# Moving 22 operand tiles of an encoder layer to staggered places in SBUF

## The chip, the cores and the metric

The kernel runs on one core of a Trainium2 chip. The metric is device time in microseconds (us) for one call; lower is better. Times of 1 ns to 1 us are given in ns.

## What is computed

One layer of a bidirectional encoder on a sequence of 256 rows of width 2048: a gated feed-forward block (FFN 1), a mixer (eight heads of attention beside a convolution, joined by one output projection), and a second feed-forward block (FFN 2). All is in float32, and nearly all the arithmetic is in large matrix products against weights that are read once:

```
h = modulate(rms_norm(x, ffn1_pre_g), sh1, sc1)
x = x + 0.5 * g1 * rms_norm(silu(h @ w_gate) * (h @ w_up) @ w_down, ffn1_post_g)
h = modulate(rms_norm(x, mix_pre_g), sh2, sc2);  proj = h @ w_in
merged = concatenate([rms_norm(attention(q, k, v)), rms_norm(conv(u))]) @ w_out
x = x + g2 * rms_norm(merged, mix_post_g)
(the second feed-forward block as the first, with sh3, sc3, g3)
```

`w_gate` and `w_up` are 2048x5632, `w_down` is 5632x2048, `w_in` 2048x5120, `w_out` 2048x2048. The nine modulation vectors come from a vector-matrix product with `w_ada`, 2048x18432.

## The kernel before, in words

**Products.** A float32 operand is split into a high and a low part, both in the type float32r, and a product is made of three: high by high, high by low, low by high. The activations stand still in TensorE's array (the stationary operand, 128x128), the weights stream past (the moving operand, 128x512). In `Group.products`, for each of the 128-deep slices k and each half t of the 256 rows, three matmuls follow each other:

```
L312  matmul(o, xh, h)     stationary: high part of the activations
L313  matmul(o, xh, l)     the same stationary operand, loaded once more
L314  matmul(o, xl, h)     stationary: low part of the activations
```

I call these three a triple. Each matmul has a weight load of its own ahead of it (PEld in the profile). A chunk of weights is two slices; `wchunk` brings it in by DMA (tile `raw`), ScalarE rounds it to `hi` (L286), and VectorE subtracts for `lo` (L287).

**Where the stationary operands lie.** The high and low parts live in tiles of 128 partitions by 4 KB, made by `slot` from the pool `work`, one place per tag: `hh0` to `hh3` and `hl0` to `hl3` hold the normalized activations (`h1`, `h2`, `h3` in tile names), four slices each; `ah0` to `ah5` and `al0` to `al5` hold the hidden activations of the feed-forward blocks (`a_0h`, `a_1l` and so on); `fs0` to `fs3` hold sums and outputs, and in the mixer the first attention parts. A slice and half start at a multiple of 512 bytes inside a tile. The tags are also reused for float32 sums, attention tiles and the convolution. The tags `ah5` and `al5` alone are larger (`SLOT` words, 4576 bytes), for the padded convolution input.

The places in the built program, as bytes in a partition modulo 256, are these. All moving operands (`hi`, `lo`) start at byte 64.

```
tag              before   after          tag          before   after
hh0 hh1 hh2 hh3    0      0 64 128 192   hl0 to hl3     0      32 96 160 224
ah0 ah1 ah2 ah3    0      0 64 128 192   al0 to al3     0      32 96 160 224
ah4                0      128            al4            0      160
ah5                0      192            al5          224      160
fs0 fs2            0      0 64           fs1 fs3        0      32 96
```

So before, the tile `al5` is the only stationary operand of a triple that is not at byte 0. It holds the low part of the last hidden block of each round of the feed-forward blocks, and stands in 128 of the 2560 triples: at the end of each pass of the down projection (line L314 with `pd_t`), in runs of eight triples.

**Order.** One engine's instructions run in the order in which the Python code issues them; the tile framework adds the waits. While products run, background lanes (`tick`) put in the modulation sums for a later block on VectorE (L190), and their transposes on TensorE.

Of the kernel before, what the change touches and what calls it, by code (L numbers as in the profile page):

```python
# [16 lines left out]
P = 128  # L17
D = 2048
S = 256
# [32 lines left out]
RAW = 7  # L52
HILO = 4
SLOT = 4 * (S + 2 * PAD)

STAGES1 = ((0, 4), (4, 8), (8, 12), (12, 16))
STAGES2 = ((0, 4), (4, 10), (10, 16))
# [3 lines left out]
def encoder_layer(ctx, tc, a, consts, out):  # L61
# [5 lines left out]
    work = ctx.enter_context(tc.tile_pool(name="work", bufs=1))  # L67
# [164 lines left out]
    def gate_tile(gc, i):  # L232

        G = [slot(f"a{p}4", [P, NT, BLK], f"G{i}{p}") for p in "hl"]
        for n in range(0, D, BLK):
            ps = tr_ps(f"psg{i}_{n}")
            for j in range(BLK // P):
                g = gc[:, n // P + j:n // P + j + 1]
                nc.tensor.matmul(ps[:, j * P:(j + 1) * P], g.to_broadcast([P, P]), ident,
                                 start=True, stop=True)  # L240
            nc.scalar.copy(G[n // MW][:, n % MW // BLK, :], ps)
        return G


    def slot(tag, shape, name, dt=F32):

        n = int(np.prod(shape[1:]))
        t = work.tile([P, SLOT if tag in ("ah5", "al5") else 4 * S], dt, tag=tag, name=name)[:, :n]
        if len(shape) == 3:
            t = t.rearrange("p (a b) -> p a b", b=shape[2])  # L250
        elif len(shape) == 4:
            t = t.rearrange("p (a b c) -> p a b c", b=shape[2], c=shape[3])
        return t

    class Parts:
# [8 lines left out]
        def put(self, n, hi, lo):  # L264
            for parts, tag, p in ((self.hi, hi, "h"), (self.lo, lo, "l")):
                parts.extend([None] * (n + 1 - len(parts)))
                parts[n] = slot(tag, [P, 4, S], f"{self.base}{p}{n}", F32R)
# [121 lines left out]
    def f_tiles(i, tags=("fs0", "fs1", "fs2", "fs3")):  # L389
        return [slot(tag, [P, NT, BLK], f"f{i}_{db}") for db, tag in enumerate(tags)]  # L390
# [557 lines left out]
```

## Time and profile before

| | before |
|---|---|
| median of three runs | 1969.43 us (1967.24 to 1972.84) |
| the profiled execution | 1970.16 us |
| its span, first to last instruction | 1968.4 us |
| TensorE busy with matmuls | 1881.0 us, 96% |
| VectorE busy | 1474.6 us, 75% |
| ScalarE busy | 932.5 us, 47% |

The profile is of one execution. Recorded matmuls overlap, since the end of one is modelled; how fast products follow each other is read from the distance between their starts, which I call the pitch. PE is TensorE, DVE VectorE, ACT ScalarE, POOL GpSimd, SP the engine that issues most transfers.

### The profile page before, as it was taken

What the parts mean: (1) busy time and instruction counts of PE and PEld (TensorE: products, weight loads), DVE (VectorE), ACT (ScalarE), POOL (GpSimd) and SP (SyncE); (2) the same over time, 40 slices, a digit from 0 to 9 for tenths busy, and PEclk for the clock granted to TensorE, in tenths of its full rate; (3) what the DMA queues carried; (4) which work ended last, traced back from release to release, by engine and by line L of the source; (5) the groups of instructions that cost most, each with busy time, mean ns of one, the idle gap of its engine ahead of it and who ended that gap; (6) DMA issues with size and microseconds to landing.
All of it is one profiled execution on the core that took longest, in us unless ns stands there. A gap on an engine that the chain in (4) does not pass through costs nothing.

```text
span 1968.4 us, 23857 instructions
## 1 busy us (share of the span) xinstructions
PE 1881.0 (96%) x8451; PEld 1534.9 (78%) x8451; DVE 1474.6 (75%) x1824; ACT 932.5 (47%) x1437; POOL 64.1 (3%) x90
## 2 busy tenths in 40 slices
PE   2999999999999999899999997999999999999997
PEld 1888887888888878688887786888888777888886
DVE  6799999777787766689997768999885455444455
ACT  3554454444444444644455656635444433444442
POOL 2000000000000000000100000000000000000000
PEclk9999999999999999899999998999999999999999
DMA  9989988999999887356655667998777666656552
GB/s 335 324 298 310 332 273 275 352 328 325 322 319 332 303 273 260 115 183 185 180 163 194 207 201 244 341 333 299 238 232 234 217 228 226 201 186 189 175 190 99
DMA packets 249431, 493.12 MB, mean 251 GB/s; under 512 B 17065, under 2 KB 42433, under 8 KB 249312
## 3 DMA queue, kind: packets, MB, share of 16 engines
q1 hardware_dynamic: 247888, 491.38, 74.8%
q8 instruction: 66, 1.08, 0.2%
q14 instruction: 53, 0.43, 0.1%
q0 software_dynamic: 1248, 0.15, 0.1%
q10 hardware_dynamic: 176, 0.07, 0.0%
HBM read 489.44 MB, written 2.10 MB: 250 GB/s over the span
## 4 chain that ended last, share of the span: by engine, by line
PE 79%; DMA 10%; DVE 6%; issue 2%; ACT 2%; POOL 0%; SPq 0%; DVEq 0%; POOLq 0%; ACTq 0%
DMA ada<-in_w_ada 8%; PE pg_t L312 8%; PE pg_t L313 8%; PE pg_t L314 8%; PE pu_t L314 7%; PE pu_t L312 7%; PE pu_t L313 7%; PE pd_t L313 6%; PE pd_t L314 6%; PE pd_t L312 6%; PE pc_t L312 2%; PE pc_t L314 2%; PE pc_t L313 2%; DVE acc L190 2%; DVE lo_d L287 2%
## 5 line engine op out<-in xcount | busy, mean ns | idle before, releaser
L190 DVE SCALAR_TENSOR_TENSOR acc<-ada,cact,acc 128x512 f32<-128x512 f32 (+2 forms) x448 | 393.4, 899 | 145.9 <-DMA ada<-in_w_ada 136.0
L286 ACT CAST hi_d<-raw_d 128x1024 fp32r<-128x1024 f32 x176 | 184.8, 1051 | 268.8 <-PE pd_t L314 220.4
L286 ACT CAST hi_g<-raw_g 128x1024 fp32r<-128x1024 f32 x176 | 185.0, 1052 | 232.3 <-PE pg_t L314 129.6
L287 DVE TENSOR_TENSOR lo_d<-raw_d,hi_d 128x1024 fp32r<-128x1024 f32 x176 | 212.4, 1223 | 107.0 <-ACT hi_d L286 106.6
L286 ACT CAST hi_u<-raw_u 128x1024 fp32r<-128x1024 f32 x176 | 184.5, 1052 | 216.0 <-PE pu_t L314 100.7
L287 DVE TENSOR_TENSOR lo_u<-raw_u,hi_u 128x1024 fp32r<-128x1024 f32 x176 | 213.3, 1222 | 84.0 <-ACT hi_u L286 83.5
L287 DVE TENSOR_TENSOR lo_g<-raw_g,hi_g 128x1024 fp32r<-128x1024 f32 x176 | 213.7, 1222 | 73.2 <-ACT hi_g L286 73.1
L313 PE MATMUL pd_t<-lo_d,a_0h 128*128 128x512 f32 x384 | 151.3, 394 | 7.2 <-DVE lo_d L287 7.2
L314 PE MATMUL pd_t<-hi_d,a_0l 128*128 128x512 f32 x384 | 151.2, 394 | 0.0
L312 PE MATMUL pd_t<-hi_d,a_0h 128*128 128x512 f32 x384 | 150.3, 393 | 0.0
L312 PE MATMUL pg_t<-hi_g,h3h 128*128 128x512 f32 x352 | 140.0, 398 | 2.0 <-ACT h3h L353 2.0
L313 PE MATMUL pg_t<-lo_g,h3h 128*128 128x512 f32 x352 | 138.5, 393 | 1.4 <-DVE lo_g L287 1.4
L312 PE MATMUL pg_t<-hi_g,h1h 128*128 128x512 f32 x352 | 139.2, 396 | 0.0
L312 PE MATMUL pu_t<-hi_u,h3h 128*128 128x512 f32 x352 | 138.8, 395 | 0.0
L312 PE MATMUL pu_t<-hi_u,h1h 128*128 128x512 f32 x352 | 138.8, 395 | 0.0
L313 PE MATMUL pu_t<-lo_u,h3h 128*128 128x512 f32 x352 | 138.0, 392 | 0.8 <-DVE lo_u L287 0.8
L314 PE MATMUL pg_t<-hi_g,h3l 128*128 128x512 f32 x352 | 138.7, 394 | 0.0
L313 PE MATMUL pg_t<-lo_g,h1h 128*128 128x512 f32 x352 | 138.4, 393 | 0.0
L314 PE MATMUL pg_t<-hi_g,h1l 128*128 128x512 f32 x352 | 138.3, 393 | 0.0
L314 PE MATMUL pu_t<-hi_u,h3l 128*128 128x512 f32 x352 | 138.3, 393 | 0.0
L314 PE MATMUL pu_t<-hi_u,h1l 128*128 128x512 f32 x352 | 138.2, 393 | 0.0
L313 PE MATMUL pu_t<-lo_u,h1h 128*128 128x512 f32 x352 | 137.9, 392 | 0.1
(257 smaller groups left out, 3601.8 us busy)
## 6 DMA issues: line engine op xcount, KB each, us to landing
ada<-in_w_ada SPq DMA_DIRECT2D x288, 512.0 KB, 5.5
raw_g<-in_ffn_w_gate SPq DMA_DIRECT2D x176, 512.0 KB, 5.0
raw_u<-in_ffn_w_up SPq DMA_DIRECT2D x176, 512.0 KB, 4.9
raw_d<-in_ffn_w_down SPq DMA_DIRECT2D x176, 512.0 KB, 5.4
raw_c<-in_w_in SPq DMA_DIRECT2D x64, 256.0 KB, 3.0
raw_q<-in_w_in SPq DMA_DIRECT2D x16, 512.0 KB, 3.8
raw_k<-in_w_in SPq DMA_DIRECT2D x16, 512.0 KB, 3.6
raw_v<-in_w_in SPq DMA_DIRECT2D x16, 512.0 KB, 3.6
```

Of the source, the lines that this page charges most:

```text
L190: nc.vector.scalar_tensor_tensor(acc, w[:, j, :], cact[:, j0 + j:j0 + j + 1], acc, op0=ALU.mult, op1=ALU.add)
L286: nc.scalar.copy(h, r)
L287: nc.vector.tensor_tensor(l, r, f32(h), op=ALU.subtract)
L312: nc.tensor.matmul(o, xh, h, start=self.first and k == 0, stop=False)
L313: nc.tensor.matmul(o, xh, l, start=False, stop=False)
L314: nc.tensor.matmul(o, xl, h, start=False, stop=self.last and k == self.nk - 1)
```

## The change

`slot` makes each tile of a tag other than `ah5` and `al5` 8 words (32 bytes) longer. The length that is used stays the same, so the tile ends in 32 unused bytes, and every later place in the pool moves on. There are 22 such tags: `hh0` to `hh3`, `hl0` to `hl3`, `ah0` to `ah4`, `al0` to `al4`, `fs0` to `fs3`. Their starts become those of the table above. Behind them, scratch tiles (`xn`, `hf`, `gs`, `ac`), `ah5`, `al5` and some constants move too, by 256 to 704 bytes. The tiles ahead of them, the weight chunks among them, stay where they were. No instruction is added, removed or moved on any engine, and every wait is the same as before.

```diff
+STAGGER = 8
...
     def slot(tag, shape, name, dt=F32):
 
         n = int(np.prod(shape[1:]))
-        t = work.tile([P, SLOT if tag in ("ah5", "al5") else 4 * S], dt, tag=tag, name=name)[:, :n]
+        t = work.tile([P, SLOT if tag in ("ah5", "al5") else 4 * S + STAGGER], dt, tag=tag,
+                      name=name)[:, :n]
```

## Rows read from the trace of the kernel before

**Rows 1.** Page: busy time of three engines, and the clock by slices.

```profile
PE 1881.0 (96%) x8451; PEld 1534.9 (78%) x8451; DVE 1474.6 (75%) x1824; ACT 932.5 (47%) x1437; POOL 64.1 (3%) x90
PEclk9999999999999999899999998999999999999999
```

**Rows 2.** Windows: stretches of the program, busy time of each engine in them.

```profile
core 0: us, PE busy (x) PEld busy (x) DVE busy (x) ACT busy (x) POOL busy (x), PEclk, DMA share, GB/s
50.00:470.00 420.00, 418.80 (x1882) 341.83 (x1881) 369.41 (x412) 206.97 (x318) 9.12 (x13) 1.00 0.91 312
830.00:1090.00 260.00, 257.83 (x1202) 212.02 (x1202) 236.00 (x415) 127.02 (x197) 14.13 (x8) 0.99 0.61 184
1550.00:1900.00 350.00, 340.26 (x1514) 276.57 (x1513) 173.44 (x157) 143.85 (x167) 0.00 (x0) 1.00 0.62 202
```

**Rows 3.** Window of the whole span, line L314 alone: the number of triples.

```profile
0.00:1968.40 1968.40, 1008.56 (x2560) 482.87 (x2560) 0.99 0.75 251
```

**Rows 4.** Windows in FFN 1's down projection; columns as in rows 2.

```profile
333.44:351.06 17.62, 17.62 (x78) 14.46 (x77) 16.01 (x15) 7.37 (x7) 0.00 (x0) 1.00 1.02 385
351.98:356.88 4.90, 4.90 (x22) 3.95 (x21) 3.37 (x3) 2.25 (x3) 0.00 (x0) 1.00 1.04 395
```

**Rows 5.** Windows in FFN 2's down projection; columns as in rows 2.

```profile
1904.95:1924.87 19.92, 19.92 (x89) 16.34 (x87) 10.46 (x10) 8.14 (x10) 0.00 (x0) 1.00 0.58 195
1925.56:1930.45 4.89, 4.89 (x22) 3.94 (x21) 2.51 (x3) 1.83 (x2) 0.00 (x0) 1.00 0.62 202
```

**Rows 6.** Timeline of PE: start, duration in us, engine, line, tiles.

```profile
351.06 0.39 PE L314 MATMUL pd_t<-hi_d,a_0l 128*128 128x512 f32 x1
351.29 0.39 PE L312 MATMUL pd_t<-hi_d,a_0h 128*128 128x512 f32 x1
351.52 0.39 PE L313 MATMUL pd_t<-lo_d,a_0h 128*128 128x512 f32 x1
351.75 0.40 PE L314 MATMUL pd_t<-hi_d,a_0l 128*128 128x512 f32 x1
351.98 0.40 PE L312 MATMUL pd_t<-hi_d,a_0h 128*128 128x512 f32 x1
...
356.88 0.40 PE L312 MATMUL pd_t<-hi_d,a_0h 128*128 128x512 f32 x1
357.12 0.39 PE L313 MATMUL pd_t<-lo_d,a_0h 128*128 128x512 f32 x1
357.35 0.39 PE L314 MATMUL pd_t<-hi_d,a_0l 128*128 128x512 f32 x1
357.58 0.39 PE L312 MATMUL pd_t<-hi_d,a_0h 128*128 128x512 f32 x1
```

**Rows 7.** Waits of PE: who was waited for, us in total, times, longest.

```profile
PE psc L204 <- DVE acc L190: 20.7, 1, 20.7
PE pst L367 <- DVE xn L364: 16.1, 2, 8.7
PE pd_t L313 <- DVE lo_d L287: 9.0, 9, 1.8
PE pg_t L312 <- ACT h3h L353: 2.0, 2, 1.1
PE pg_t L313 <- DVE lo_g L287: 1.4, 2, 1.0
```

**Rows 8.** Lines L630 and L354 on DVE: duration ns min/median/max, first and last start.

```profile
L630 DVE SCALAR_TENSOR_TENSOR co<-uTh,cw,co x120: 473/476/485, 849.4 to 931.4; 128x256 f32<-128x256 f32 x120
L354 DVE TENSOR_TENSOR a_0l<-pa,a_0h x24: 680/684/692, 268.7 to 1482.6; 128x512 fp32r<-128x512 f32 x24
```

## The prediction

> **What bounds the kernel now.** I read the page first: TensorE is busy 96% of the span at full clock but for two dips, VectorE 75% [rows 1]. A busy TensorE can hide waits, so I read stretches next. In the middle of FFN 1, in the mixer and in FFN 2, TensorE is busy 97 to 99.7% of each stretch, while DVE is at 88%, 91% and 50% and the DMA share goes from 0.91 to 0.61 [rows 2]. Where the other engines and the transfers are half idle, the products come no faster. So the kernel's time is the number of products times their pitch, and what the change can do is worth what it does to that pitch: there are 2560 triples, 7680 products [rows 3], and one ns in the pitch is 7.7 us.
>
> The pitch is then read where no product waits. In a stretch of FFN 1's down projection in which every stationary operand starts at byte 0, 77 products take 17.62 us, 228.8 ns each; in FFN 2 87 take 19.92 us, 229.0 ns [rows 4, 5]; these are the first row of each group, and the count is that of the weight loads, one per step from start to start. The traffic beside it is twice as dense in the first (385 GB/s against 195), and the pitch is the same, so transfers don't set it.
>
> **The one place that shows the operand of this change.** The tile `al5` starts at byte 224, all others at 0. It comes in runs of eight triples, in each of which two loads are from byte 0 and one is from byte 224. In such a run 21 products take 4.90 us, 233.3 ns each, and in the other block 4.89, again 233 (the second rows of [rows 4, 5]). That is 4.5 ns more per product, 13.5 ns per triple. I looked where it begins. At 351.29 the high part of this tile, `ah5`, has taken over, at byte 0 and in the same far part of the memory as `al5`, and the steps stay 0.23 us; from the product ahead of the first one on `al5` (351.52) they go to 0.23, 0.23, 0.24 in turn, 0.70 us per triple in place of 0.69 [rows 6]. The step from 356.88 to 357.12 is still 0.24, though both operands there are again `h` tiles at byte 0; behind it the old rhythm is back. So the loss hangs on the load at another byte and on the way back from it, neither on the far tile as such nor on the tile's length, which `ah5` shares.
>
> **The change part by part.** No instruction, wait or transfer is added or moved; only places change.
>
> *Triples.* After the change each low part lies 32 bytes behind its high part (`al5` and `ah5`: 32 bytes ahead, as now modulo 256). So every triple goes 32 bytes away and back, which today 128 triples do. If going away and coming back cost what they cost at `al5`, 2560 - 128 = 2432 triples become 13.5 ns longer: +32.8 us. In which direction the step goes first can't matter to the sum if the cost depends on the difference of two successive places, because each triple holds one step of each sign. The bounds from the same row: nothing, if it is something else about byte 224; and for each single load that is not at byte 0 the whole 13.5 ns, since one such load made a triple that much longer. After the change 2560 low loads and 1968 of the 2560 high operands, which are loaded twice, are off byte 0: 6496 loads, 128 of them so already. That is +6368 x 13.5 ns = +86 us. I take the first value, because the row has that pattern itself; and at the step back to byte 0 it shows a cost on a load that is at byte 0, which speaks for the difference and against the place.
>
> *Steps from tile to tile.* Every eight triples the next tile begins, a further 32 bytes on. These are one step in 24, at the price of half a round trip already counted above, so nothing is added.
>
> *What hides it.* Little. Products wait for `lo`, `hi` or an activation tile for some 14 us in all (9.0 + 2.0 + 1.4 are the largest) [rows 7]; slower products give VectorE more time there, and I let a third of it, 5 us, go. The 20.7 and 16.1 us ahead of the first products are before TensorE's stream begins and stay.
>
> *Other engines.* VectorE, ScalarE and GpSimd read and write the moved tiles. The convolution reads `uTh` at 31 offsets, 4 bytes apart, so at all kinds of places: 473 to 485 ns over 120 instructions. The splits into `al0` to `al5`, five of these at byte 0 and one at 224, take 680 to 692 ns [rows 8]. So a place costs these engines nothing that could be seen, at most 12 ns on an engine that is not the bound. Transposes and attention read moved tiles too; they are too few to count.
>
> Sum against the profiled execution: 1970.2 + 32.8 - 5 = 1998 us. The median of the runs shown is 0.7 us below that execution, so I predict 1997 us, +1.4%.
>
> **A rule that speaks against this.** The rows say that where a stationary operand starts moves the pitch of products by 4.5 ns [rows 4]. The Trainium skill, page "SBUF — State Buffer", section "Who interferes with whom", gives TensorE two independent read ports, one for the moving operand and one for weight loads, which wait for no one; by that rule a place can cost nothing, and the sum would be 1970. The run of `al5` doesn't fit it, so it only lends its number to the rival "no change" below. The page "TensorE: Matmul & The Clock Gate", section "Back-to-back issue gap", gives 512 / 2.4 + 2.5 ns for an isolated product, about 216; by that figure some 13 ns per product, 99 us in all, would be there to be won if a better place existed. No row here shows a product that fast.
>
> **The rivals.**
>
> *No change (1970 us).* The loss at `al5` could come from a step down modulo 256, or from byte 224 against the moving operand's byte 64, and a step of 32 up could cost nothing. For it: only one pair of bytes has been seen. Against it: every triple also steps back down. Chance 0.10.
>
> *Each load off byte 0 pays (2033 to 2050 us).* The upper bound above gives 1970 + 86 - 5 = 2051. If a start at a multiple of 128 is as good as one at 256, the high parts at bytes 64 and 192 (1312 of 2560) pay and the others don't: 2560 + 2 x 1312 - 128 = 5056 loads, +68 us, 2033. For it: the profile can't tell a bad place from a bad difference with certainty. Chance 0.20.
>
> *Half the price (1980 to 1988 us).* The part of the loss that comes at the way out and the part that comes at the way back are not equal in the rows, and a run could absorb one of them: +16 us. Chance 0.09.
>
> *Faster (about 1937 us).* Today's 229 ns may itself hold a stall between the weight load and the moving read that run at the same time, both at fixed places, 0 and 64. Eight places could make that stall rarer, as `al5` makes it worse. Priced as the mirror image, 4.5 ns less per product in the 7296 products of the 2432 triples, this is -33 us. It decides as soon as the mean pitch falls under 228.8 ns. For it: the pitch is not explained by anything else in the trace. Against it: the only other place seen is worse. Chance 0.15.
>
> **How the numbers follow.** The forecast (1988 to 2008) has chance 0.46; half the price 0.09, off byte 0 pays 0.20, no change 0.10, faster 0.15. So slower by more than 0.3% has 0.75, within 0.3% has 0.10, faster 0.15; 0.3%, 6 us, is about what runs that lie 5.6 us apart can tell. The range reaches from the edge of no change, 1965, to the upper bound, 2050; outside are the faster case and a little above. The likeliest case by itself is 1988 to 2008.
>
> **What would show it.** In the profile after: the same 8451 matmuls; a pitch near 233 ns in dense stretches of all three blocks; in the runs of `ah5` and `al5`, which keep their difference, 233 as before; TensorE at 96% or more, and waits for `lo` a little shorter. A pitch still near 229 everywhere is the rival "no change"; triples of 700 ns only where the high part is at byte 0, and of 727 ns where it is not, speak for the second rival; a pitch under 228 for the last. I would be wrong if the pitch depended on where the load stands against the moving operand, for then `al5` would be one sample of eight.

## The result: 1.05% slower, and the profile after

The median went from 1968.34 us (four runs, the three of the table above and one more) to 1987.35 us (four runs, 1983.89 to 1990.83). The ratio is 1.0105, with a 95% interval of 1.0087 to 1.0123: +19 us, where +28 was forecast. The profiled execution took 1990.83 us, 20.7 more than that of before, with the same 8451 matmuls.

The page after, to be read against [rows 1]; TensorE's and VectorE's busy time, and the clock:

```profile
PE 1906.1 (96%) x8451; PEld 1536.5 (77%) x8451; DVE 1476.7 (74%) x1824; ACT 932.5 (47%) x1437; POOL 63.0 (3%) x90
PEclk9999999999999999899999998999999999999999
```

TensorE's matmul time rose by 25.1 us. The weight loads' own busy time hardly moved (1534.9 before, 1536.5 now), and neither did VectorE's (1474.6 and 1476.7) and ScalarE's (932.5 in both). So the loss is in the pitch. Four neighbouring windows in FFN 2's up projection after the change hold 24 products each, one pair of tiles each: high and low parts at bytes 0 and 32, 64 and 96, 128 and 160, 192 and 224. The fifth is the run on `ah5` and `al5`, 21 products, that answers to the second row of [rows 4]. Columns are those of rows 2:

```profile
1749.57:1755.13 5.56, 5.56 (x26) 4.51 (x25) 2.45 (x2) 2.59 (x3) 0.00 (x0) 1.00 0.56 169
1755.13:1760.72 5.59, 5.59 (x25) 4.50 (x24) 2.45 (x2) 2.10 (x2) 0.00 (x0) 1.00 0.69 211
1760.72:1766.28 5.56, 5.56 (x26) 4.51 (x24) 2.45 (x2) 2.10 (x2) 0.00 (x0) 1.00 0.61 187
1766.28:1771.89 5.61, 5.61 (x26) 4.51 (x25) 2.75 (x3) 2.09 (x2) 0.00 (x0) 1.00 0.63 189
356.03:360.93 4.90, 4.90 (x23) 3.94 (x21) 3.60 (x4) 2.73 (x4) 0.00 (x0) 1.00 1.04 396
```

At the pitch of before at byte 0, 24 products take 5.49 us (24 x 228.8 ns, [rows 4]). Now they take 5.56, 5.59, 5.56 and 5.61, that is 231.7, 232.9, 231.7 and 233.8 ns, and the run of the last tile is as it was, 4.90 us. So each of these four pairs of places is worse than byte 0 was, and not all by the same amount. The counts of touched instructions in brackets are one or two above 24, since a window also counts what only reaches into it.

A few waits became shorter. The waits of PE after, as in [rows 7]:

```profile
PE pd_t L316 <- DVE lo_d L290: 7.7, 7, 1.9
PE pg_t L315 <- ACT h3h L356: 2.0, 2, 1.1
PE pg_t L316 <- DVE lo_g L290: 0.7, 1, 0.7
```

These gave back 2 us (9.0 to 7.7 and 1.4 to 0.7). All of TensorE's idle time, its span less its busy time, went from 87.4 us (1968.4 - 1881.0) to 82.9 us (1989.0 - 1906.1), so 4.5 us of the 25.1 were covered.

### The profile page after: what moved, and what is told of

Read it like the earlier page. It is cut to its first block, busy times and chain, and to the rows that moved or that the text cites. A ratio compares the mean times of both kernels' runs of the same rounds, so it can differ in the third digit from the quotient of the medians.

```text
span 1989.0 us, 23857 instructions
## 1 busy us (share of the span) xinstructions
PE 1906.1 (96%) x8451; PEld 1536.5 (77%) x8451; DVE 1476.7 (74%) x1824; ACT 932.5 (47%) x1437; POOL 63.0 (3%) x90
## 4 chain that ended last, share of the span: by engine, by line
PE 48%; DMA 5%; DVE 3%; issue 1%; ACT 1%; POOL 0%; DVEq 0%; POOLq 0%; ACTq 0%
DMA ada<-in_w_ada 5%; PE pg_t L316 4%; PE pg_t L315 4%; PE pg_t L317 4%; PE pu_t L315 4%; PE pu_t L316 4%; PE pu_t L317 4%; PE pd_t L316 3%; PE pd_t L315 3%; PE pd_t L317 3%; PE pc_t L315 2%; PE pc_t L316 2%; PE pc_t L317 2%; DVE lo_d L290 1%; PE pq_t L316 1%
## 5 line engine op out<-in xcount | busy, mean ns | idle before, releaser
L290 DVE TENSOR_TENSOR lo_g<-raw_g,hi_g 128x1024 fp32r<-128x1024 f32 x176 | 213.8, 1222 | 78.9 <-ACT hi_g L289 78.4
```

The source lines that it names most:

```text
L290: nc.vector.tensor_tensor(l, r, f32(h), op=ALU.subtract)
```

## The experiments

Two theories stood at the start, both with a cost at `al5`. Theory D is the forecast's: a product pays when the weight load steps to another byte than the load before it. Theory P is the second rival: each load off byte 0 pays for itself. Theory M came in beside them: what counts is where the load stands against the moving operand. Theory A, a later rival of M, is that the byte of the load counts by itself.

### All stationary operands at one byte, and one step

Six kernels differ from before in this edit, with other numbers in the call of `places`; `gap(n, ...)` leaves `n` words unused. The edit places all high tiles first and then all low tiles, with a gap of `first` words ahead of all and of `step` words between the two, and makes `al5` end on a 256-byte line:

```diff
-SLOT = 4 * (S + 2 * PAD)
+SLOT = 4 * (S + 2 * PAD) + 8
...
+    def places(first, step):
+        his = [f"hh{i}" for i in range(4)] + [f"ah{i}" for i in range(6)] + ["fs0", "fs2"]
+        los = [f"hl{i}" for i in range(4)] + [f"al{i}" for i in range(6)] + ["fs1", "fs3"]
+        gap(first, "gap0")
+        for tag in his:
+            slot(tag, [P, 4 * S], f"at_{tag}")
+        gap(step, "gap1")
+        for tag in los:
+            slot(tag, [P, 4 * S], f"at_{tag}")
...
+    places(0, 0)
     hT = Parts("h1", "h", range(4))
```

`places(0, 0)`, every operand at byte 0:

> All high tiles lie one after another, then all low tiles, every one at byte 0 of a 256-byte line, al5 too. Theory D (a product pays when its weight load starts at another byte than the load before): no triple has a step, so every triple takes 687 ns, the 128 of al5 too, -1.7 us against before, about 1967 us. Theory P (each load off byte 0 pays): the same. Both fall if the far order of the tiles, new here, moves the pitch by itself.

It took 1960.74 us against 1960.65 of before on the same chip, 0.9999 (0.9990 to 1.0009), at 228.9 ns. So moving the tiles by many KB shows no cost beyond 0.1% as long as the byte in the line stays.

`places(8, 0)`, every operand at byte 32:

> As all_0, but every stationary operand of the products at byte 32. Theory D: still no step between loads, 687 ns per triple, about 1967 us. Theory P: three loads per triple off byte 0, at 13.5 ns each 727 ns per triple, about +100 us, 2065 us. Theory M (what counts is where the load stands against the moving operand at byte 64): some other pitch than 229 ns, in either direction.

It took 1982.53 us, 1.0110 (1.0094 to 1.0125). Windows of 24 products in FFN 2, first of `all_0`, then of `all_32`, columns as above:

```profile
1730.89:1736.38 5.49, 5.49 (x25) 4.51 (x24) 2.45 (x2) 2.09 (x2) 0.00 (x0) 1.00 0.65 193
```

```profile
1735.02:1740.62 5.60, 5.60 (x25) 4.50 (x24) 2.45 (x2) 2.69 (x3) 0.00 (x0) 1.00 0.65 189
1740.62:1746.22 5.60, 5.60 (x25) 4.50 (x24) 2.45 (x2) 2.58 (x3) 0.00 (x0) 1.00 0.58 163
```

5.60 us is 233.3 ns per product, 700 per triple, with no step between loads anywhere. **Theory D falls.** Theory P falls too: three loads off byte 0 cost 13.5 ns in a triple, no more than the one load at `al5` did, not 40. What is left is that a place is good or bad, in itself (A) or against the moving operand (M).

`places(0, 8)` and `places(0, 56)`, high parts at 0, low parts at 32 and at 224:

> High tiles at byte 0, low tiles at byte 32: each triple steps 32 bytes up and back, without the walk from tile to tile that the change has. Theory D: as the change's tiles at 0 and 32, 695 to 700 ns per triple, 2560 x 8 to 13 ns less some 5 us of waits, 1984 to 1997 us. Theory P: one load off byte 0 per triple, 700 ns, the upper end. If steps up alone are dear and steps down free, or the walk matters, it leaves this band.

> High tiles at byte 0, low tiles at byte 224, so every triple has the places that the runs of al5 had before. Both theories: 700 ns per triple everywhere, 2560 x 13.3 = +34 us against all_0, less some 5 to 8 us of waits, about 1993 us. If the cost of al5 hung on its place far up in the memory, 687 ns and 1967 us.

They took 1975.61 us, 1.0079 (1.0063 to 1.0095), and 1983.06 us, 1.0114 (1.0099 to 1.0129). Both times lie below what was expected, which was reckoned from a chip on which before took 1968 us; against before on their own chip they are +15 us, the lower end of what 8 to 13 ns per triple less 5 us make, and +22 us, where +26 to +29 was expected. From the start of one triple to the next, without those that wait (over 720 ns), the first has a mean of 695 ns, going to and fro between stretches of 700 and of 693, and the second 700. A window of 24 products in the second:

```profile
1734.01:1739.61 5.60, 5.60 (x26) 4.51 (x24) 2.45 (x2) 2.69 (x3) 0.00 (x0) 1.00 0.65 187
```

This is the pitch of `al5` in all tiles, so `al5` was no matter of its place far up in the memory. A step of 32 bytes up and one of 32 bytes down do not cost the same.

### The byte against the moving operand's byte

A kernel of products alone, in runs of 48 in the pattern of a triple, all in one trace at full clock. It computes nothing of the layer:

```python
def run(bh, bl, m):
    ps = psum.tile([P, 512], F32, tag="mm", name=f"c_{bh}_{bl}_{m}")
    for n in range(N):
        k = n // 3 % 16
        t, b = (hi, bh) if n % 3 < 2 else (lo, bl)
        j = 2 * (n // 3 % 4) + (n % 3 == 1)
        nc.tensor.matmul(ps, t[:, b + k * P:b + (k + 1) * P],
                         mov[:, m + j * 512:m + (j + 1) * 512], start=n == 0, stop=n == N - 1)
```

> Products alone, in runs of 48 (16 triples of the kernel's pattern) without any other work, so the output is not the layer: stationary operands at each of eight bytes (0 to 224 in steps of 32) against the moving operand at each of eight bytes; then high and low parts at every pair of bytes with the moving operand at 64; then eight finer bytes. Theory A (the place of the load by itself): the pitch is 229 ns at byte 0 and 233 at byte 32 whatever the moving operand's byte. Theory M (the place against the moving operand): the pitch depends on the difference of the two bytes, so 0 against 64 and 32 against 96 both give 229, and 32 against 64 gives 233. The old theory D, which all_32 has thrown out, would give 229 wherever high and low parts are at the same byte.

Six of its runs as windows of 42 products; stationary and moving byte are 0 and 0, 64 and 64, 192 and 0, 0 and 64, 32 and 96, 32 and 64. The columns after PEld are ACT, POOL, the clock and the DMA's:

```profile
32.23:41.75 9.52, 9.52 (x43) 7.88 (x42) 0.00 (x0) 0.00 (x0) 1.00 0.01 2
232.59:242.11 9.52, 9.52 (x43) 7.88 (x42) 0.00 (x0) 0.00 (x0) 1.00 0.00 0
99.13:108.74 9.61, 9.61 (x44) 7.89 (x42) 0.00 (x0) 0.00 (x0) 1.00 0.00 0
210.41:220.02 9.61, 9.61 (x43) 7.89 (x42) 0.00 (x0) 0.00 (x0) 1.00 0.01 2
310.67:320.29 9.62, 9.62 (x44) 7.89 (x42) 0.00 (x0) 0.00 (x0) 1.00 0.00 0
221.42:231.22 9.80, 9.80 (x44) 7.87 (x43) 0.00 (x0) 0.00 (x0) 1.00 0.00 0
```

The pairs with the same difference agree: 226.7 ns twice (9.52 / 42), 228.8 to 229.0 three times (9.61 and 9.62), and 233.3 for the last. The recorded time of the loads is 7.9 us in all of them, so a load's duration in the profile doesn't show the effect. All 64 runs with high and low parts at the same byte, pitch in ns from the start of the 7th product to that of the 46th in each:

```
              stationary byte
moving byte   0      32     64     96     128    160    192    224
  0          226.7  233.4  233.4  234.2  232.4  233.3  228.9  233.3
 32          233.3  226.8  233.4  233.4  234.2  232.4  233.3  228.9
 64          228.9  233.4  226.7  233.4  233.4  234.2  232.4  233.3
 96          233.3  228.9  233.3  226.7  233.4  233.4  234.2  232.4
128          233.2  233.3  228.9  233.3  226.7  233.4  233.4  234.2
160          234.3  232.2  233.3  228.9  233.3  226.7  233.4  233.4
192          233.3  234.2  232.4  233.3  228.9  233.3  226.7  233.4
224          233.4  233.4  234.2  232.4  233.3  228.9  233.3  226.7
```

Each row is the one above it, moved on by one place, to 0.1 ns but for the difference 128, which gave 232.2 to 232.4 seven times and 233.2 once. So where all three loads of a triple are at one byte, the difference of the two bytes modulo 256 sets the pitch, and neither byte alone does. Before, the difference was 0 - 64, that is 192: the second best of eight. The same trace, with the moving operand at 64 and high and low parts apart as in the change, gave 231.0 (0 and 32), 233.3 (64 and 96), 231.1 (128 and 160), 233.2 (192 and 160) and 233.4 ns (192 and 224), and 233.3 for 0 and 224, the places of `al5` before.

Where the two parts are at different bytes, the pitch is not the mean of what each byte gives alone. Four windows of 42 products, moving operand at 64; high and low byte are 128 and 128, 160 and 160, 128 and 160, 0 and 96:

```profile
1145.13:1154.93 9.80, 9.80 (x43) 7.90 (x42) 0.00 (x0) 0.00 (x0) 1.00 0.00 0
265.88:275.72 9.84, 9.84 (x43) 7.91 (x42) 0.00 (x0) 0.00 (x0) 1.00 0.01 2
1156.33:1166.03 9.70, 9.70 (x43) 7.89 (x42) 0.00 (x0) 0.00 (x0) 1.00 0.01 2
777.89:787.51 9.62, 9.62 (x43) 7.89 (x42) 0.00 (x0) 0.00 (x0) 1.00 0.00 0
```

Bytes 128 and 160 together take 231 ns, less than either alone (233.3 and 234.3), and 0 with 96 takes 229, no more than 0 alone, though 96 alone takes 233.4. So the places of the loads of a triple also act together, and theory M gives no sum for such triples. All triples of the change are of this kind: their pitch is measured here, not derived. Of the 64 pairs of high and low byte with the moving operand at 64, one is faster than byte 0 (64 and 64, 226.7 ns), four take 228.9 to 229.0, among them byte 0 itself, and the other 59 take 229.9 to 235.3.

> Products alone again (not the layer): the moving operand at byte 0, stationary operands at each of 64 places 4 bytes apart; then the moving operand of the middle product of a triple, the low weights, at another byte than the high ones; then the two outer orders of a triple. Theory M (difference of load and moving operand modulo 256): the multiples of 32 give the same values as in the first scan, 226.7, 233.4, 233.4, 234.2, 232.4, 233.3, 228.9, 233.3 ns; the places between are open, 52 bytes below gave 226.7 and 44 bytes below 236.7. If a place without any stall exists, some value near 216 ns should turn up; if 226.7 is the floor of a product with its load, nothing is below it.

Here seven of the eight multiples of 32 repeated to 0.1 ns, and nothing came out under 226.7. Several differences between them reach it (120, 132, 144, 156, 228, 252 bytes). Three places did not agree between the scans: a difference of 128 gave 232.4 in the first and 233.5 in this one, 204 gave 226.7 and 235.7, 208 gave 231.8 and 233.3. So for some differences there is more than one rhythm. Two windows of 42 products of this trace, both at a difference of 128:

```profile
388.81:398.62 9.81, 9.81 (x44) 7.89 (x43) 0.00 (x0) 0.00 (x0) 1.00 0.01 2
789.61:799.37 9.76, 9.76 (x44) 7.91 (x42) 0.00 (x0) 0.00 (x0) 1.00 0.00 0
```

They take 233.6 and 232.4 ns with the same bytes. With the moving operand of the middle product at a byte of its own nothing came under 228.9 ns, and the other order of a triple gave the same values (226.7, 228.9, 233.4).

### The layer with the operands at other differences

`places(16, 0)` and `places(32, 0)`, all at byte 64 and all at byte 128:

> Every stationary operand of the products at byte 64, the byte of the moving operands. If starts at a multiple of 64 are good: 687 ns per triple and 1961 us, as all_0. Theory M: a new difference, a pitch other than 229, between 225 and 238 ns. The change's tiles at 64 with low parts at 96 took 699 ns per triple.

> Every stationary operand at byte 128. In the change, tiles at 128 and 160 took 695 ns per triple, like those at 0 and 32, while those at 64 and 192 took 699 to 701. If the period is 128 bytes, byte 128 is byte 0: 687 ns and 1961 us. If the whole 256 bytes count, some other pitch.

They took 1948.56 us, 0.9936 (0.9916 to 0.9955), and 1984.9 us, 1.0120 (1.0098 to 1.0142). Byte 128 is no byte 0; a period of 128 bytes is out. Byte 64 is better than byte 0. To tell whether 64 is good by itself, the weights were moved in place of the stationary operands:

```diff
+    wpool.tile([P, 48], F32, tag="gap", bufs=1, name="gapw")
+    work.tile([P, 16], F32, tag="gap", name="gapk")
```

> The kernel before with two unused gaps, so that the weight chunks, the moving operands, start at byte 0 in place of 64, and the stationary operands stay at byte 0 (al5 at 224). Theory M: difference 0 in nearly all triples, 680 ns each as in all_64, about 0.993 of before. Theory A (only the load's own byte counts): nothing changes, 687 ns, and all_64 was fast because byte 64 is good in itself.

It took 1946.86 us, 0.9935 (0.9921 to 0.9949). 24 products of it in FFN 2 take 5.44 us, 226.7 ns:

```profile
1728.71:1734.15 5.44, 5.44 (x26) 4.51 (x24) 2.45 (x2) 2.11 (x2) 0.00 (x0) 1.00 0.70 196
```

Theory A falls: stationary operands that had not moved at all in their line became faster because the weights came to the same byte. Last, the smallest edit that puts all operands at 64, in the tile order of before:

```diff
-SLOT = 4 * (S + 2 * PAD)
+SLOT = 4 * (S + 2 * PAD) + 8
...
+    work.tile([P, 16], F32, tag="gap", name="gap")
```

> The kernel before with one unused gap of 64 bytes ahead of the pool, and al5 on a 256-byte line: every stationary operand of the products at byte 64, where the moving operands are, with the tiles in the order of before. Theory M: 680 ns per triple in all 2560, the same as all_64, 0.993 to 0.994 of before, about 1947 us; the time falls by 128 x 13 + 2432 x 6.5 ns = 17.5 us less what new waits for the low weights take back, some 3 to 5 us.

It took 1949.3 us, 0.9937 (0.9922 to 0.9952): faster than before, where the change was slower. 24 products of it in FFN 2:

```profile
1723.46:1728.90 5.44, 5.44 (x26) 4.50 (x24) 2.45 (x2) 2.11 (x2) 0.00 (x0) 1.00 0.64 195
1728.90:1734.34 5.44, 5.44 (x26) 4.50 (x24) 2.66 (x3) 2.11 (x2) 0.00 (x0) 1.00 0.66 193
```

5.44 us is 226.7 ns, the value of the scan. Of the 17.5 us that the pitch is worth, 12 arrived. The traces show two places for the other 5: triples without a wait take 681.0 ns in the mean, not 680, since a few take 692 to 696 (1 ns x 2560 is 2.6 us), and TensorE's idle time is 81.4 us against 78.9 in `all_0`. The second is an estimate, as `all_0` ran on another chip.

## Why the prediction was right, and where it was not

**The bound** was right. The time of the layer followed the pitch in every run, up and down.

**The sign, and the place of the loss,** were right: the pitch in all dense stretches rose, and the run of `al5` stayed at 233.3 ns.

**The time was met partly by luck.** 1987.35 us lies 0.65 us below the likeliest case (1988 to 2008) and inside the band of the rival "half the price" (1980 to 1988). The forecast spread the cost of one pair of places over all, by a mechanism that does not hold; that most other pairs cost about as much could not be read from that one.

**The mechanism was wrong.** The step that failed is "so the loss hangs on the load at another byte and on the way back from it", and with it the choice of the first value "because the row has that pattern itself". `all_32` has no way out and back, and its triples take 700 ns as well. The row could not tell a step from a place: in the only sample, the load that differed from its neighbours was also the only one with another distance to the weights. The step from 356.88 to 357.12, on which I threw out the place, can as well be read as a rhythm that takes one more product to settle. What stands in its place is the last sentence of the prediction: the pitch depends on where the load stands against the moving operand, and `al5` was one sample. `weights_at_0` shows it in the layer (226.7 ns without a move of the stationary operands in their line), the table for all eight differences. Byte 0 against 64 is one of the two good ones, and 59 of the 64 pairs of places are slower, so spreading the operands had to lose unless it found one of the few others. That byte 0 was good is luck of where the weights lie. How the places of two different loads in a triple act together stays open. Had the weights lain at byte 32, byte 0 would have been at 233.3 ns already, by the table.

**The size of the term.** 2432 triples at +13.5 ns, 32.8 us, was too much. By the scan's pairs the change's mean pitch is (592 x 231.0 + 592 x 233.3 + 656 x 231.1 + 128 x 233.2 + 592 x 233.4) / 2560 = 232.2 ns, against (2432 x 228.9 + 128 x 233.3) / 2560 = 229.1 before: 3.1 ns x 7680 = 24 us. That `al5`'s loss was taken for every pair is the 9 us too much; about half of the triples (592 + 656 of 2560) are at 231.

**The cover.** 5 us were let go for shorter waits. That was the right size: TensorE's busy time rose by 25.1 us and its idle time fell by 4.5. Only about half of it is in the waits for `lo` that the prediction named; the rest is spread over other waits.

**Other engines** were rightly put at nothing: DVE's busy time went from 1474.6 to 1476.7 us.

**The rivals.** "No change" is out: with a triple at one byte, places at multiples of 32 bytes differ by up to 7.6 ns per product (226.7 to 234.3). The rule of two independent read ports that the prediction takes from the Trainium skill (page "SBUF — State Buffer", section "Who interferes with whom") foresees no such difference, and here the measurement decides. "Each load off byte 0 pays" is out by `all_32`. "Half the price" has the number by chance: its reason, that one of the two steps of a triple is absorbed, falls with the step, for `all_32` has none. "Faster" came closest to the cause, since it put the cost between the load and the moving read at fixed places, but it had the wrong average; its gain is real where all operands sit at the moving operand's byte, and stops at 226.7 ns. That a stall lies behind it is not shown. The 216 ns of the Trainium skill for an isolated product (page "TensorE: Matmul & The Clock Gate", section "Back-to-back issue gap") were reached in none of the 267 runs of products in the two scans.

## What to carry to other kernels

Where float32r products are the bound, read their pitch in dense stretches and compare tiles by their place in a 256-byte line: a single tile that is 4 ns off is a free experiment. It tells that places matter, not how; two samples can't separate a step, a place and a distance, and a scan of products alone, one run, can. For the pattern of this kernel, give stationary and moving operands the same byte modulo 256; one or two unused gaps won 0.6% here. For other shapes and types no run here shows it, so scan first.

## What was not expected of the hardware

With a 128x128 float32r load for each 128x512 product, and all loads of a triple at one byte, the pitch takes values from 226.7 to 234.3 ns at multiples of 32 bytes by the difference of two start addresses modulo 256. They repeat to 0.1 ns but for the difference 128 (232.2 to 233.5). With the other engines idle the values are those of the layer, at the four differences tried in both (0, 64, 192, 224). The recorded duration of a load, 187 to 190 ns in the mean of each run of products, does not show the effect. Why a difference of 0 or 192 bytes is good is not shown by these runs.
